# Layer 1 feed-forward of a two-layer diffusion backbone: seven block products for gate and up, down summed in PSUM

## The chip, the core and the metric

The kernel runs on one core of one Trainium2 chip. The time is the device time of an execution in microseconds (us), the median of several runs. The engines are TensorE (PE, matmuls), VectorE (DVE), ScalarE (ACT), GpSimd (POOL) and the DMA queues, here all issued from SyncE (SP). Each engine goes through its own list of instructions in order and waits on semaphores for the others.

## The reference

A network of two layers on 512 latent tokens and 256 context tokens of width 1024, all in float32. Layer 0 mixes tokens by differential attention, layer 1 by grouped-query attention; behind each stands a gated feed-forward of hidden width 2816. Only the latent tokens leave layer 1, so its feed-forward runs on 512 tokens:

```
def swiglu(t, w_gu, w_down):
    gate, up = jnp.split(t @ w_gu, 2, axis=-1)
    return (jax.nn.silu(gate) * up) @ w_down
```

Its input `t` is the RMS-normed and modulated residual stream `x`, and its output is multiplied by a gate vector and added to `x`.

## The kernel before

Every float32 matrix is split into a high part (a cast to the matmul's type) and a low part (source minus high part), and every product is three matmuls, high x high, high x low and low x high. The high parts are cast on ACT, the low parts are subtracted on POOL (weights) or DVE (activations).

`ffn` (L369) serves both layers. The hidden width is cut in 22 chunks of 128 columns, worked in 11 pieces of two. For a chunk, `load` fetches 1 MB of gate and up weights into one of three raw buffers, `stage` splits them (ACT L86, POOL L93), and `gu_mm` sums gate and up over eight blocks of the width for all 512 tokens (L433: 2 x 8 x 3 matmuls of 512 columns; the first two chunks go in halves of 256 columns, since the last token block isn't normed yet when they start). ACT applies silu (L478), DVE multiplies by up (L479), ACT and DVE split the result (L490, L493). `down` then multiplies a piece by its two blocks of w_down (L100 to L102, through `mm3`), for each of four token blocks and two halves of the width, and DVE multiplies each result by the gate vector (L386) and adds it to `x` (L387): 88 such pairs in layer 1. PSUM is three pools of two buffers: S (two banks each), P and T (one bank each).

Ahead of it stands the output projection of the attention (L361, L365 on DVE). After each token block `mk_after` starts the norm (`norm_a`, scaling on L297), and one block later `norm_b` transposes it (L307), modulates it (L322 on DVE, L324 on ACT) and splits it into `h3` (L327, L328). The last block's norm is finished inside `ffn`, by the callback `mid` after the first products of chunk 0. `store` (L1133) writes the output.

The program is written in this order, but a scheduler rearranges it for each engine by its own estimate of times (`schedule_with_timeline_sim=True`, L1180), so the order of rows on an engine is read from the built program, not from the code.

## Time and profile before

| | us |
|---|---|
| median of 3 runs | 1746.75 (1746.62 to 1749.67) |
| span of the profiled execution | 1742.5 |
| median less span | 4.25 |
| TensorE busy | 1657.0 (95%) |
| VectorE, GpSimd, ScalarE busy | 1237.5, 767.6, 673.0 |
| layer 1's feed-forward, first unbroken matmul to end | 1366.6 to 1742.5 |

The page counts the busy time of each engine over the whole span. To judge one stage one goes to views cut to its stretch: windows (busy time in a stretch), groups by line, the timeline of one engine, and the chain of waits, which is followed back from the last instruction. A matmul's own duration in the timeline is longer than its pace, because matmuls overlap; the pace is read from the distance of starts. The clock that TensorE was granted stands as a share of full speed: 1.00 is 2.4 GHz, 0.50 is 1.2 GHz.

### The profile page before, as it was taken

What the parts mean: (1) busy time and instruction counts of PE and PEld (TensorE: products, weight loads), DVE (VectorE), ACT (ScalarE), POOL (GpSimd) and SP (SyncE); (2) the same over time, 40 slices, a digit from 0 to 9 for tenths busy, and PEclk for the clock granted to TensorE, in tenths of its full rate; (3) what the DMA queues carried; (4) which work ended last, traced back from release to release, by engine and by line L of the source; (5) the groups of instructions that cost most, each with busy time, mean ns of one, the idle gap of its engine ahead of it and who ended that gap; (6) DMA issues with size and microseconds to landing.
All of it is one profiled execution on the core that took longest, in us unless ns stands there. A gap on an engine that the chain in (4) does not pass through costs nothing.

```text
span 1742.5 us, 23575 instructions
## 1 busy us (share of the span) xinstructions
PE 1657.0 (95%) x8934; PEld 1403.6 (81%) x8934; DVE 1237.5 (71%) x2016; ACT 673.0 (39%) x1491; POOL 767.6 (44%) x702
## 2 busy tenths in 40 slices
PE   5899999989998999999999999999999999999998
PEld 2789899975778888887777888778897888888887
DVE  4777888877484488878777555798883467677676
ACT  4667767677444121111211022364673522222120
POOL 2687666664645242223232233174435344354340
PEclk8899999999999999999999999999999999999999
DMA  8311111129523133355333221021203133233311
GB/s 303 102 55 38 46 46 58 34 75 336 195 73 121 49 121 111 107 169 169 122 119 99 73 73 40 25 74 48 73 25 120 36 105 103 73 97 99 95 49 49
DMA packets 162435, 165.81 MB, mean 95 GB/s; under 512 B 5097, under 2 KB 120186, under 8 KB 162322
## 3 DMA queue, kind: packets, MB, share of 16 engines
q1 hardware_dynamic: 162322, 164.31, 29.5%
q8 instruction: 70, 1.15, 0.3%
q14 instruction: 43, 0.35, 0.1%
HBM read 159.81 MB, written 4.48 MB: 94 GB/s over the span
## 4 chain that ended last, share of the span: by engine, by line
PE 68%; DVE 18%; ACT 4%; DMA 4%; POOL 3%; issue 2%; SPq 0%; DVEq 0%; ACTq 0%; POOLq 0%
PE psgu L433 24%; PE psgc L433 5%; PE psd L100 5%; PE psd L102 5%; PE psd L101 5%; DVE adacc L225 3%; DMA adaw<-in_ada_w_dram 3%; PE psp L100 2%; PE psp L102 2%; PE psp L101 2%; DVE adacc L223 2%; DVE x L387 2%; DVE xd L386 1%; PE pso L100 1%; PE pso L102 1%
## 5 line engine op out<-in xcount | busy, mean ns | idle before, releaser
L93 POOL TENSOR_TENSOR gul<-gu,guh 128x2048 fp32r<-128x2048 f32 x44 | 211.6, 4809 | 419.6 <-ACT guh L86 419.6
L386 DVE TENSOR_TENSOR xd<-psd,gate 128x512 f32<-128x512 f32 x220 | 151.1, 687 | 202.7 <-PE psd L102 202.5
L387 DVE TENSOR_TENSOR x<-x,xd 128x512 f32<-128x512 f32 x220 | 274.4, 1249 | 5.5
L86 ACT CAST guh<-gu 128x2048 fp32r<-128x2048 f32 x44 | 83.9, 1906 | 403.8 <-PE psgu L433 234.4
L91 POOL TENSOR_TENSOR dl<-wd,dh 128x1024 fp32r<-128x1024 f32 x44 | 120.9, 2768 | 146.1 <-ACT dh L86 146.1
L433 PE MATMUL psgu<-h3latl,guh 128*128 128x512 f32 (+1 forms) x384 | 144.5, 377 | 1.1 <-POOL h3latl L328 1.1
L433 PE MATMUL psgu<-h3lath,gul 128*128 128x512 f32 (+1 forms) x384 | 144.4, 376 | 0.0
L433 PE MATMUL psgu<-h3lath,guh 128*128 128x512 f32 (+1 forms) x384 | 144.3, 377 | 0.0
L433 PE MATMUL psgu<-h2lath,guh 128*128 128x512 f32 (+1 forms) x368 | 142.1, 386 | 0.0
L433 PE MATMUL psgu<-h2lath,gul 128*128 128x512 f32 (+1 forms) x368 | 141.8, 385 | 0.0
L433 PE MATMUL psgu<-h2latl,guh 128*128 128x512 f32 (+1 forms) x368 | 141.8, 385 | 0.0
L100 PE MATMUL psd<-dh,ah 128*128 128x512 f32 x264 | 106.0, 402 | 16.2 <-DVE xd L386 12.1
L102 PE MATMUL psd<-dh,al 128*128 128x512 f32 x264 | 104.8, 397 | 0.0
L101 PE MATMUL psd<-dl,ah 128*128 128x512 f32 x264 | 104.5, 396 | 0.0
L433 PE MATMUL psgc<-h2ctxh,gul 128*128 128x256 f32 x352 | 100.2, 285 | 0.4 <-POOL gul L93 0.4
L433 PE MATMUL psgc<-h2ctxh,guh 128*128 128x256 f32 x352 | 100.1, 284 | 0.0
L433 PE MATMUL psgc<-h2ctxl,guh 128*128 128x256 f32 x352 | 99.6, 283 | 0.0
L225 DVE SCALAR_TENSOR_TENSOR adacc<-adaw,cond,adacc 128x512 f32<-128x512 f32 x112 | 97.5, 896 | 1.3
L100 PE MATMUL psp<-dwh,h0lath 128*128 128x384 f32 x256 | 88.9, 347 | 7.6 <-DVE vl L97 7.6
L101 PE MATMUL psp<-dwl,h0lath 128*128 128x384 f32 x256 | 88.9, 347 | 0.0
L102 PE MATMUL psp<-dwh,h0latl 128*128 128x384 f32 x256 | 88.8, 347 | 0.0
L433 PEld LDWEIGHTS psgu<-h3latl,guh 128*128 128x128 f32 x384 | 72.2, 188 | 15.8 <-POOL h3latl L328 1.3
(389 smaller groups left out, 4669.1 us busy)
## 6 DMA issues: line engine op xcount, KB each, us to landing
adaw<-in_ada_w_dram SPq DMA_DIRECT2D x48, 1024.0 KB
gu<-in_ffn_w_gu_dram SPq DMA_DIRECT2D x88, 512.0 KB
wd<-in_ffn_w_down_dram SPq DMA_DIRECT2D x22, 1024.0 KB
dw<-in_diff_w_in_dram SPq DMA_DIRECT2D x48, 256.0 KB
x<-in_x_dram SPq DMA_DIRECT2D x8, 512.0 KB
wo<-in_diff_w_out_dram SPq DMA_DIRECT2D x4, 1024.0 KB
gw<-in_gqa_w_in_dram SPq DMA_DIRECT2D x4, 1024.0 KB
wo<-in_gqa_w_out_dram SPq DMA_DIRECT2D x4, 1024.0 KB
```

Of the source, the lines that this page charges most:

```text
L86: S.copy(hi, src)
L91: G.tensor_sub(lo[:, ns], src[:, ns], hi[:, ns])
L93: G.tensor_sub(lo[:, :, ns], src[:, :, ns], hi[:, :, ns])
L100: PE.matmul(ps, lhi, rhi, start=start, stop=False)
L101: PE.matmul(ps, lhi, rlo, start=False, stop=False)
L102: PE.matmul(ps, llo, rhi, start=False, stop=stop)
L223: V.tensor_scalar(acc, w[:, k, :], c, None, op0=ALU.mult)
L225: V.scalar_tensor_tensor(acc, w[:, k, :], c, acc, op0=ALU.mult, op1=ALU.add)
L386: V.tensor_mul(tmp, ps, gates[g][:, s, cs])
L387: last_v[0] = V.tensor_add(xt[tb][:, cs], xt[tb][:, cs], tmp)
L433: last[0] = PE.matmul(o, w_[:, k, us], act.t[kind][x_].k(k, sl_), start=(k == 0 and x_ == 0 and w_ is whi), stop=(k == KC - 1 and w_ is wlo))
```

## The change

Only layer 1's feed-forward changes in what it does. Layer 0 and both attentions keep their code, but for the order of two buffers.

`ffn` is replaced by `ffn_up` and `ffn_down`. For gate and up the tokens are cut in two halves of 256 (blocks 0 and 1, blocks 2 and 3), the width in two halves of 512, and the two output halves are gate and up. The 2 x 2 by 2 x 2 block product is made of seven products (Strassen's, in Winograd's form) in place of eight. Weight operands: four blocks as they are and three sums (`prep`, L583 and L584 on POOL, L586 and L588 on DVE). Token operands: b11, b21, b22 as they are and the combinations t1 to t4, which need blocks of both halves (`Forms.done`, L371 to L376, all on DVE). Each operand is split in high and low: for weights L594 on ACT, L595 on DVE (on POOL for product 4); for tokens L351 on ACT, L352 on DVE or POOL. A product is 12 matmuls of 256 columns (L626). The results are put together while they accumulate in PSUM (copies L632, L637, L639 and silu L635, L642 on ACT; L634, L641, L644, L645, L648 on DVE). Products 1 and 2 of chunks 0 to 2 stand ahead of the last norm (`product_order`, `mid` at `None`). The gated activations are written to DRAM (`put`).

`ffn_down` then goes over all 22 chunks twice, once per half of the tokens: it reads the activations back (four chunks at a time), splits them (L669, L670), loads w_down two chunks at a time, splits it (L678 on ACT, L679 on POOL), and sums over all chunks in PSUM, so that the gate multiply and the add to `x` (L702, L703) come once for each block and half of the width.

```diff
+        def done(self, xs, tb, banks=None):
+            ht = norm_mod(xs, norm_t(xs, tb, self.l, 1, banks), tb, self.l, 1)
+            half = 0 if tb in self.halves[0] else 1
+            j = self.halves[half].index(tb)
+            lo, hi = ht[:, 0:4, :], ht[:, 4:8, :]
+            self.ht[half, j] = (lo, hi)
+            if half == 0:
+                self.put("b11", j, lo, V)
+                self.put("b21", j, hi, G)
+            else:
+                b11, b21 = self.ht[0, j]
+                self.put("b22", j, hi, G)
+                V.tensor_sub(b11, lo, b11)
+                self.put("t1", j, b11, V)
+                V.tensor_sub(lo, hi, lo)
+                V.tensor_sub(hi, hi, b11)
+                self.put("t2", j, hi, G)
+                V.tensor_sub(b21, b21, hi)
+                self.put("t3", j, lo, V)
+                self.put("t4", j, b21, G)
...
+    RHS = {1: "b11", 2: "b21", 3: "b22", 4: "t4", 5: "t1", 6: "t2", 7: "t3"}
+    PLEAD = 7
+
+    def product_order():
+        o = [(0, 1), (0, 2), (1, 1), (1, 2), None, (2, 1), (2, 2), (0, 5), (0, 6), (0, 3), (0, 7), (1, 5), (0, 4), (1, 6), (1, 3), (1, 7)]
+        o += [(1, 4), (2, 5), (2, 6), (2, 3), (2, 7)]
+        for h in range(3, NHC):
+            o += [(h, 1), (h - 1, 4), (h, 2), (h, 5), (h, 6), (h, 3), (h, 7)]
+        return o + [(NHC - 1, 4)]
...
+        def prep(hc, n):
+            w = raw[hc]
+            r11, r12, r21, r22 = [w[:, k : k + 4, u : u + P] for u in (0, P) for k in (0, 4)]
+            s1 = st_tile(hc)
+            if n == 5:
+                adds[0].tensor_add(s1, r21, r22)
+                adds[1].tensor_sub(r21, r11, r21)
+            elif n == 6:
+                adds[2].tensor_sub(r11, s1, r11)
+            elif n == 3:
+                adds[3].tensor_sub(r12, r12, r11)
+            src = {1: r11, 2: r12, 5: s1, 6: r11, 3: r12, 7: r21, 4: r22}[n]
+            if not wq:
+                t = slab("w", F32R, f"wf{l}_{hc}_{n}", 2).rearrange("p a (x k n) -> p a x k n", x=2, k=4)
+                wq.extend([t[:, 0], t[:, 1]])
+            t = wform[hc, n] = wq.pop(0)
+            S.copy(t[:, 0], src)
+            (G if n == 4 else V).tensor_sub(t[:, 1], src, t[:, 0])
+            if n == 4:
+                load(hc + 3)
...
+            w, x = wform.pop((hc, n)), F.tiles[RHS[n]]
+            for k in range(4):
+                for a_, b_ in ((0, 0), (0, 1), (1, 0)):
+                    last_m[0] = PE.matmul(
+                        ps, w[:, a_, k, :], x[:, b_, k, :],
+                        start=(n in (1, 2, 5) and k == 0 and a_ + b_ == 0),
+                        stop=(k == 3 and a_ == 1), skip_group_check=n in (3, 4, 6, 7))
+            c1, c2, c5, g1, g2, u2 = [ev[hc][:, e * th : e * th + th] for e in range(6)]
+            if n == 1:
+                S.copy(c1, ps)
+            elif n == 2:
+                V.tensor_add(g1, ps, c1)
+                S.activation(g1, g1, AF.Silu)
+            elif n == 5:
+                S.copy(c5, ps)
+            elif n == 6:
+                S.copy(c2, ps)
+            elif n == 3:
+                V.tensor_add(g2, ps, c2)
+                S.activation(g2, g2, AF.Silu)
+            elif n == 7:
+                V.tensor_add(u2, ps, c5)
+                last_v[0] = V.tensor_mul(g2, g2, u2)
+                puts.append((i, hc, 1, g2))
+            else:
+                last_v[0] = V.tensor_mul(g1, g1, ps)
+                puts.append((i, hc, 0, g1))
...
+                if k % 4 == 0:
+                    n = min(4, NHC - k)
+                    r = raw_tile(f"ar{l}_{half}_{k}", 4, th)[:, :n]
+                    dma(r, a_dram[k : k + n, :, half, :].rearrange("k p n -> p k n"))
+                    t = a_tile(half, k).rearrange("p (x k n) -> p x k n", x=2, k=4)
+                    S.copy(t[:, 0, :n], r)
+                    V.tensor_sub(t[:, 1, :n], r, t[:, 0, :n])
+                    for e in range(n):
+                        aw[k + e] = (t[:, 0, e], t[:, 1, e])
+                if k % 2 == 0:
+                    r = raw_tile(f"wd{l}_{half}_{k}", 2, D)
+                    dma(r, w_down[l, k * P : (k + 2) * P, :].rearrange("(k p) n -> p k n", p=P))
+                    ww["raw"] = r
+                t = slab("w", F32R, f"wd{l}_{half}_{k}x", 2)
+                S.copy(t[:, 0], ww["raw"][:, k % 2])
+                lo_eng.tensor_sub(t[:, 1], ww["raw"][:, k % 2], t[:, 0])
+                ww[k] = (t[:, 0], t[:, 1])
...
+            def out(tb, ch):
+                s = 0 if tb < NLAT else 1
+                cs = slice(ch * 512, ch * 512 + 512)
+                tmp = xtp.tile([P, 512], F32, tag="xtmp", name=f"xd{l}_{tb}_{ch}")
+                V.tensor_mul(tmp, ps[tb][ch], gates[g][:, s, cs])
+                last_v[0] = V.tensor_add(xt[tb][:, cs], xt[tb][:, cs], tmp)
+                after(tb, ch)
...
-    h3 = Act("h3", ("dd", "ee"))
-    after = mk_after(1, 1, h3, 1, ("f", "xc"), NLAT - 1)
+    HALVES1 = ([0, 1], [2, 3])
+    TH1 = 2 * P
+    form1 = lambda n, t: slab(t, F32R, f"hf1{n}", 2).rearrange("p x (k n) -> p x k n", k=4)
+    F1 = Forms(1, HALVES1, {n: form1(n, t) for n, t in (("b11", "e"), ("b21", "e"), ("b22", "g"), ("t1", "g"), ("t2", "d"), ("t3", "d"), ("t4", "k"))})
+    after = mk_after(
+        1, 1, slots(["xc", "f"], "11"), lambda xs, tb: F1.done(xs, tb), 1, NLAT - 1)
     out_proj(wto, wtags, xt, oT1, lat, gw_out[0], gates[1, 0], "1", after, {})
-    tags1 = dict(gu="gk", a=None, al="l", sil="l")
+    st1 = slab("k", F32, "st1").rearrange("p (s k n) -> p s k n", s=4, k=4)
+    a1 = dram.tile([NHC, P, 2, TH1], F32, name="a1")
+    ffn_up(
+        1, F1, lambda hc: slab("l", F32, f"ev1_{hc}"), lambda hc: st1[:, hc % 4], a1, (G, G, V, V),
+        lambda: after(None, True))
...
-    ffn(1, xt, h3, lat, (1, 1), tags1, lambda: after(None, True), None, [], store)
+    ffn_down(
+        1, xt, HALVES1, (1, 1), a1, lambda half, k: slab("l", F32R, f"a21_{half}_{k}"),
+        (("S", "S"), ("P", "T")), G, lambda half, k: None, store)
```

The order of the rows. The names: `wf_h_n` is the split weight operand of chunk h (a tile holds two operands), `gu_h` its raw weights, `st` the tile of sums, `psu` and `psc` PSUM, `ev` the evacuated results, `hf1b` and `hf1t` the split token operands.

First DVE at the start of the feed-forward. Before, from the last add of the projection to the last block's low halves:

```order
L365 TENSOR_TENSOR x_6176<-x_6176,xo_13492 128x512
L322 TENSOR_SCALAR xs11xc<-pt_13543,modA,mod_128 128x128 x4
L328 TENSOR_TENSOR h3latl_13151<-xs11f,h3lath_13149 128x4x128
L112 TENSOR_SCALAR m_n_13497<-ss_13495 128x1
L328 TENSOR_TENSOR h3latl_13151<-xs11xc,h3lath_13149 128x4x128
L105 TENSOR_TENSOR m_n_13497<-m_n_13497,r_n_13498 128x1
L106 SCALAR_TENSOR_TENSOR m_n_13497<-m_n_13497,r_n_13498 128x1
L107 SCALAR_TENSOR_TENSOR r_n_13498<-m_n_13497,r_n_13498 128x1
L297 TENSOR_SCALAR xs11xc<-x_6176,r_n_13498 128x1024
L322 TENSOR_SCALAR xs11xc<-pt_13565,modA,mod_128 128x128 x4
L328 TENSOR_TENSOR h3latl_13151<-xs11xc,h3lath_13149 128x4x128
L479 TENSOR_TENSOR sil_13717<-sil_13717,psgu_0_13518 128x512
```

After, in the middle of the same stretch, with the last block's modulation (L325) and the rows up to t1's last low half (the last row; `hf1t_13151` is t1):

```order
L325 TENSOR_SCALAR xs_0_13436<-pt_13644,modA,mod_128 128x128 x3
L595 TENSOR_TENSOR wf_0_3_13559<-gu_0_13511,wf_0_3_13559 128x512
L325 TENSOR_SCALAR xs_0_13436<-pt_13644,modA,mod_128 128x128
L595 TENSOR_TENSOR wf_1_5_13595<-st_13509,wf_1_5_13595 128x512
L376 TENSOR_TENSOR xs_1_13335<-xs_1_13335,xs_0_13436 128x512
L371 TENSOR_TENSOR xs_1_13335<-xs_0_13436,xs_1_13335 128x512
L595 TENSOR_TENSOR wf_1_6_13682<-gu_1_13514,wf_1_6_13682 128x512
L634 TENSOR_TENSOR ev_2_13687<-psu_2b,ev_2_13687 128x256
L595 TENSOR_TENSOR wf_1_6_13682<-gu_1_13514,wf_1_6_13682 128x512
L373 TENSOR_TENSOR xs_0_13436<-xs_0_13436 128x512
L352 TENSOR_TENSOR hf1t_13153<-xs_0_13436,hf1t_13153 128x4x128
L352 TENSOR_TENSOR hf1t_13151<-xs_1_13335,hf1t_13151 128x4x128
```

Weight operands, evacuations and combinations of tokens now stand in one row with the last norm.

Next PE at the start. Before, around the transposes of the last block:

```order
L433 MATMUL psgu_1_13620<-h3latl_13151,guh_1_13616 128x256
L433 MATMUL psgu_1_13620<-h3lath_13149,gul_1_13617 128x256
L307 MATMUL pt_13565<-ident,xs11xc 128x128 x4
L307 MATMUL pt_13570<-ident,xs11xc 128x128 x4
L433 MATMUL psgu_1_13620<-h3lath_13149,guh_1_13616 128x256
```

After, the same place (`pt_13644` and `pt_13649` are the last block's transposes):

```order
L626 MATMUL psu_0_13543<-hf1b_13149,wf_0_1_13520 128x256 x12
L626 MATMUL psu_1_13578<-hf1b_13149,wf_1_1_13525 128x256 x12
L310 MATMUL pt_13644<-ident,xs_0_13436 128x128 x4
L626 MATMUL psu_2a<-hf1b_13148,wf_2_1_13530 128x256
L310 MATMUL pt_13649<-ident,xs_0_13436 128x128 x4
L626 MATMUL psu_2a<-hf1b_13148,wf_2_1_13530 128x256 x5
L626 MATMUL psc_0_13721<-hf1t_13151,wf_0_5_13537 128x256
L626 MATMUL psc_1_13793<-hf1t_13151,wf_1_5_13595 128x256
L626 MATMUL psc_0_13721<-hf1t_13151,wf_0_5_13537 128x256 x11
```

Behind the last product of chunk 2 that needs the first half of the tokens, the next row already needs t1 (`hf1t_13151`).

Last DVE in the middle of the loop. Before, beside chunks 16 and 17:

```order
L479 TENSOR_TENSOR sil_13717<-sil_13717,psgu_16_15251 128x512
L386 TENSOR_TENSOR xd_7_0_1_15326<-psd_7_0_1_15319,gate_12144 128x512
L387 TENSOR_TENSOR x_6173<-x_6173,xd_7_0_1_15326 128x512
L493 TENSOR_TENSOR a_8_15302<-sil_13717,a_8_15302 128x512
L386 TENSOR_TENSOR xd_7_1_0_15336<-psd_7_1_0_15329,gate_12144 128x512
L387 TENSOR_TENSOR x_6173<-x_6173,xd_7_1_0_15336 128x512
L386 TENSOR_TENSOR xd_7_1_1_15346<-psd_7_1_1_15339,gate_12144 128x512
L387 TENSOR_TENSOR x_6173<-x_6173,xd_7_1_1_15346 128x512
L386 TENSOR_TENSOR xd_7_2_0_15356<-psd_7_2_0_15349,gate_12144 128x512
L387 TENSOR_TENSOR x_6176<-x_6176,xd_7_2_0_15356 128x512
```

After, beside chunks 11 to 13:

```order
L648 TENSOR_TENSOR ev_11_14957<-ev_11_14957,psu_11_14956 128x256
L595 TENSOR_TENSOR wf_13_2_15094<-gu_13_14829,wf_13_2_15094 128x512
L595 TENSOR_TENSOR wf_13_2_15094<-st_13509,wf_13_2_15094 128x512
L588 TENSOR_TENSOR gu_13_14829<-gu_13_14829 128x4x128
L595 TENSOR_TENSOR wf_13_6_15130<-gu_13_14829,wf_13_6_15130 128x512
L641 TENSOR_TENSOR ev_12_15080<-psc_12_15134,ev_12_15080 128x256
L595 TENSOR_TENSOR wf_13_6_15130<-gu_13_14829,wf_13_6_15130 128x512
L644 TENSOR_TENSOR ev_12_15080<-psu_12_15079,ev_12_15080 128x256
L645 TENSOR_TENSOR ev_12_15080<-ev_12_15080 128x256
L595 TENSOR_TENSOR wf_13_7_15164<-gu_13_14829,wf_13_7_15164 128x512
L595 TENSOR_TENSOR wf_13_7_15164<-gu_14_14953,wf_13_7_15164 128x512
L634 TENSOR_TENSOR ev_13_15204<-psu_13_15203,ev_13_15204 128x256
```

The residual's multiplies and adds are gone from the loop; low halves of weights (L595) stand in their place, and between them rows that wait for a product in PSUM.

## Rows read from the trace of the kernel before

**Rows 1.** The page: busy us, share of the span and instructions of each engine.
```profile
PE 1657.0 (95%) x8934; PEld 1403.6 (81%) x8934; DVE 1237.5 (71%) x2016; ACT 673.0 (39%) x1491; POOL 767.6 (44%) x702
```

**Rows 2.** Timeline of PE, start of layer 1's feed-forward: start, us, then line and operation.
```profile
1366.62 0.39 PE L433 MATMUL psgu<-h3latl,guh 128*128 128x256 f32 x1 [1.11 <-POOL h3latl L328]
1366.84 0.28 PE L433 MATMUL psgu<-h3lath,gul 128*128 128x256 f32 x1
...
1372.53 0.28 PE L433 MATMUL psgu<-h3lath,gul 128*128 128x256 f32 x1
```

**Rows 3.** Timeline of PE, its last matmul.
```profile
1737.67 0.40 PE L102 MATMUL psd<-dh,a 128*128 128x512 f32 x1
```

**Rows 4.** Windows, layer 1's feed-forward: us, busy by engine (instructions), PEclk, DMA share, GB/s.
```profile
1430.00:1700.00 270.00, 270.00 (x1159) 217.31 (x1158) 192.28 (x162) 63.75 (x64) 120.34 (x34) 1.00 0.30 89
```

**Rows 5.** Chain of waits in 1560 to 1600: shares by line, then start, us, what.
```profile
by line: PE psgu L433 71.8%; PE psd L102 9.9%; PE psd L101 9.3%; PE psd L100 9.3%
...
1560.14 9.80 PE psgu L433 x42
```

**Rows 6.** Tile h3latl, one operation on two engines: min/median/max ns, first and last start.
```profile
L328 POOL TENSOR_TENSOR h3latl<-xs11f,h3lath x2: 1290/1504/1717, 1357.7 to 1364.8; 128x512 fp32r<-128x512 f32 x2
L328 DVE TENSOR_TENSOR h3latl<-xs11f,h3lath x2: 680/680/680, 1359.4 to 1366.6; 128x512 fp32r<-128x512 f32 x2
...
L328 DVE TENSOR_TENSOR h3latl<-xs11xc,h3lath x2: 1360/1366/1371, 1368.9 to 1377.6; 128x512 fp32r<-128x512 f32 x2
```

**Rows 7.** Timelines of DVE and of POOL around 1560 to 1579.
```profile
1562.36 5.70 POOL L91 TENSOR_TENSOR dl<-wd,dh 128x1024 fp32r<-128x1024 f32 x2
1571.77 4.62 POOL L93 TENSOR_TENSOR gul<-gu,guh 128x2048 fp32r<-128x2048 f32 x1 [3.72 <-ACT guh L86]
...
1562.90 0.68 DVE L386 TENSOR_TENSOR xd<-psd,gate 128x512 f32<-128x512 f32 x1
1572.10 4.84 DVE L387 TENSOR_TENSOR x<-x,xd 128x512 f32<-128x512 f32 x1
1578.17 0.69 DVE L387 TENSOR_TENSOR x<-x,xd 128x512 f32<-128x512 f32 x1
1578.78 0.69 DVE L493 TENSOR_TENSOR a<-sil,a 128x512 fp32r<-128x512 f32 x1
```

**Rows 8.** Groups by line in 1430 to 1700: count, busy us, mean ns, idle before.
```profile
L387 DVE TENSOR_TENSOR x<-x,xd 128x512 f32<-128x512 f32 x64 | 118.3, 1848 | 1.7
```

**Rows 9.** Line L97, a DVE subtraction that reads PSUM, 128x256.
```profile
L97 DVE TENSOR_TENSOR oT1latl<-pgo,oT1lath x16: 411/425/427, 1233.8 to 1324.1; 128x256 fp32r<-128x256 f32 x16
```

**Rows 10.** Timeline of DVE between the last projection and the last block's modulation.
```profile
1364.03 0.68 DVE L361 TENSOR_TENSOR xo<-pso,gate 128x512 f32<-128x512 f32 x1
1370.76 0.75 DVE L297 TENSOR_SCALAR xs11xc<-x,r_n 128x1024 f32<-128x1024 f32 x1
1374.60 1.37 DVE L322 TENSOR_SCALAR xs11xc<-pt,modA,mod 128x128 f32<-128x128 f32 x4 [3.08 <-PE pt L307]
```

**Rows 11.** PE's idle at 528.8 (timeline) and the granted clock behind it (windows).
```profile
533.67 0.69 PE L307 MATMUL pt<-ident,xs01f 128*128 128x128 f32 x2 [4.87 <-DVE m_n L112]
539.00:540.00 1.00, 1.00 (x7) 1.00 (x7) 1.00 (x3) 1.00 (x4) 0.04 (x1) 0.50 0.00 0
541.00:542.00 1.00, 1.00 (x11) 1.00 (x10) 0.50 (x1) 1.00 (x2) 0.97 (x1) 1.00 0.00 0
800.00:810.00 10.00, 7.31 (x38) 5.92 (x37) 5.44 (x5) 2.77 (x3) 4.56 (x1) 1.00 0.60 214
```

**Rows 12.** A load of 1 MB and its cast, two splits (timelines), a crowded stretch (windows).
```profile
624.40 0.99 SPq L55 DMA_DIRECT2D gu<-in_ffn_w_gu_dram  x2
630.12 1.91 ACT L86 CAST guh<-gu 128x2048 fp32r<-128x2048 f32 x1 [9.47 <-DMA gu<-in_ffn_w_gu_dram]
1318.83 4.77 POOL L91 TENSOR_TENSOR dl<-wd,dh 128x1024 fp32r<-128x1024 f32 x2 [5.90 <-ACT dh L86]
400.00:410.00 10.00, 10.00 (x74) 6.04 (x76) 7.85 (x20) 7.30 (x20) 9.41 (x19) 1.00 1.03 370
```

More of the change, by code (lines that the diff above doesn't have):

```diff
@@ L298, in norm_a, with norm_t @@
         return xs
-    def norm_t(xs, tb, l, which):
+    def norm_t(xs, tb, l, which, banks=None):
         pts = []
@@ L303, in norm_t @@
             nm = f"pt{l}{which}{tb}{q}"
-            pt = psb(nm, "T") if q or l + which == 2 else ps2(nm)[:, 0, :]
+            if banks:
+                pt = psb(nm, banks)
+            else:
+                pt = psb(nm, "T") if q or l + which == 2 else ps2(nm)[:, 0, :]
             pts.append(pt.rearrange("p (k n) -> p k n", n=P))
@@ L308, in norm_t, with norm_mod @@
         return pts
-    last_v, last_s = [None], [None]
-    def norm_m(xs, src, tb, l, which, hi, lo, nv=4):
+    last_v, last_s, last_m = [None], [None], [None]
+    def norm_mod(xs, src, tb, l, which, nv=4):
         s = 0 if tb < NLAT else 1
@@ L324, in norm_m @@
                         S.activation(ht[:, k, :], x_, AF.Identity, bias=b, scale=a)
+        return ht
+    def norm_m(xs, src, tb, l, which, hi, lo, nv=4):
+        ht = norm_mod(xs, src, tb, l, which, nv)
         for q in range(2):
@@ L328, in norm_m, with norm_b, __init__, put @@
             last_v[0] = (V if q else G).tensor_sub(lo.q(q), ht[:, qs, :], hi.q(q))
-    def norm_b(xs, tb, l, which, hi, lo):
-        norm_m(xs, norm_t(xs, tb, l, which), tb, l, which, hi, lo)
+    def norm_b(xs, tb, l, which, hi, lo, banks=None):
+        norm_m(xs, norm_t(xs, tb, l, which, banks), tb, l, which, hi, lo)
+    class Forms:
+        def __init__(self, l, halves, tiles):
+            self.l, self.halves, self.tiles, self.ht, self.late = l, halves, tiles, {}, []
+        def put(self, name, j, src, eng):
+            if name not in self.tiles:
+                self.late.append((name, j, src, eng))
+                return
+            t, cs = self.tiles[name], slice(j * P, j * P + P)
+            S.copy(t[:, 0, :, cs], src)
+            last_v[0] = eng.tensor_sub(t[:, 1, :, cs], src, t[:, 0, :, cs])
+        def rest(self, tiles):
+            self.tiles.update(tiles)
+            for a in sorted(self.late, key=lambda a: a[0]):
+                self.put(*a)
+        def done(self, xs, tb, banks=None):
[18 more added lines that the diff above has]
+                self.put("t4", j, b21, G)
     def o_weights(wt, tags, w_dram, nm, ch):
@@ new lines, in ffn_down, with prep, mms @@
+    def ffn_down(l, xt, halves, g, a_dram, a_tile, banks, lo_eng, step, after):
+        th = len(halves[0]) * P
+        for half, tbs in enumerate(halves):
+            items, aw, ww = [], {}, {}
+            def prep(k):
+                if k >= NHC:
+                    return
+                if k % 4 == 0:
[15 more added lines that the diff above has]
+                ww[k] = (t[:, 0], t[:, 1])
+            for k in range(3):
+                prep(k)
+            ps = {}
+            for j, tb in enumerate(tbs):
+                b = banks[half][j]
+                if b == "S":
+                    t = ps2(f"psd{l}_{tb}")
+                    ps[tb] = [t[:, 0, :], t[:, 1, :]]
+                else:
+                    ps[tb] = [psb(f"psd{l}_{tb}_{ch}", b) for ch in range(2)]
+            def mms(k, tb, ch):
+                j = tbs.index(tb)
+                ts_, cs = slice(j * P, j * P + P), slice(ch * 512, ch * 512 + 512)
+                mm3(ps[tb][ch], aw[k][0][:, ts_], aw[k][1][:, ts_], ww[k][0][:, cs], ww[k][1][:, cs], k == 0, k == NHC - 1)
+            def out(tb, ch):
[5 more added lines that the diff above has]
+                after(tb, ch)
+            TAIL = 2
+            for k in range(NHC - TAIL):
+                prep(k + 3)
+                for tb in tbs:
+                    for ch in range(2):
+                        mms(k, tb, ch)
+                step(half, k)
+            for tb in tbs:
+                for ch in range(2):
+                    for k in range(NHC - TAIL, NHC):
+                        mms(k, tb, ch)
+                    out(tb, ch)
```

68 lines of the change are left out of this document (55 added, 13 removed).

## The prediction

> **What bounds the kernel now.** I read the page first: TensorE (PE) is busy 95% of the span and VectorE (DVE) 71% [rows 1]. Those shares are averages over stages, so I went to the stage that is changed, the feed-forward of layer 1. Its unbroken run begins at 1366.62 us, with an L433 matmul behind a wait of 1.1 us [rows 2], and its last matmul starts at 1737.67 [rows 3]. In 1430 to 1700 the windows view has PE busy 270.00 of 270 us, DVE 192.28, ACT 63.75, POOL 120.34, DMA at 89 GB/s [rows 4], and the chain of waits there consists of matmuls only [rows 5]. So PE sets the time of this stage, 371.5 us (1366.62 to about 1738.1), and every other engine has slack, DVE 78 us in 270.
>
> The engines beside PE matter all the same, because the change hands them work. Here the reader should look at pairs of rows. A subtraction of 128x512 with both inputs in SBUF takes 0.68 us on DVE and 1.29 on POOL when alone; begun during the other's, DVE's takes 1.36 and POOL's 1.72 [rows 6]. The residual add `x<-x,xd` (two SBUF inputs) takes 0.69 us in the quiet and 4.84 beside a POOL operation of 4.62, but `xd<-psd,gate`, whose first input is PSUM, takes 0.68 us at 1562.90, in the middle of POOL's 1562.36 to 1568.06 [rows 7]. I read this as: a DVE operation on two SBUF inputs and a POOL operation exclude each other, and a DVE operation that reads PSUM is free. That is how L387 comes to a mean of 1848 ns here [rows 8].
>
> **What the change takes from PE.** Before, a chunk of the hidden width costs 2x8x3 = 48 matmuls of 512 columns at 0.2333 us (42 in 9.80 us [rows 5]): 11.2 us. After, seven products of 4x3 = 12 matmuls of 256 columns, 84 in all. Their pace, each with new weights, stands in the startup of before: 48 steps from 1366.84 to 1372.53 [rows 2], 0.1186 us, so 9.96 a chunk. The first two chunks of before run at 256 columns already (96 x 0.1186 = 11.4 each). Over 22 chunks 246.8 becomes 219.1. Down is 528 matmuls of 512 columns in both kernels, 123.2 us. PE's bare sum, with 0.9 us of transposes: 343.2 us against 371.5, less 28.
>
> **What it adds in the up loop: forms and evacuations.** By the order of rows two chunks cost DVE 26 operations: 16 of 128x512 on two SBUF inputs (12 low halves L595, the additions L586 and L588), 2 of 128x256 in SBUF (L645) and 8 of 128x256 from PSUM (L634, L641, L644, L648). Back to back the first kind paces 0.61 us (1578.17 to 1578.78 [rows 7]): 9.8; the PSUM kind lasts 0.425 [rows 9]: 3.4; the L645 have no row, I take them at 0.4, between half of 0.69 and a PSUM one: 0.8. POOL gets six of 128x512 (L583, L584, one L595 a chunk): 6 x 1.29 = 7.7. If nothing coincides that is 21.7 us; if all eight PSUM reads lie beside POOL, 18.3; PE needs 19.92. So DVE and POOL together, with much of their time free before, become as long as PE. Neither bound is reached, since the engines wait for each other at short distance: L648 waits for a chunk's last product and frees the bank that PE wants one product (1.42 us) later, L644 and L634 two products, and each stands in DVE's row among forms. I take 20.65, a little above the middle of 18.3 and 21.7: 0.7 more than PE, over the 10.6 pairs left after the first six products 7.5 us of PE idle (bounds 0 and 18.9). ACT isn't in question: 7 casts a chunk, each a quarter of the tile that takes 1.91 [rows 12], three copies and two activations.
>
> **What it adds at the start: a hole.** Six products (chunks 0 to 2, operands b11 and b21) need token blocks 0 and 1 only; all others need t1 to t4 or b22, which exist only once block 3 is normed, transposed, modulated and combined. Before, the last `xo` multiply starts at 1364.03, block 3 is scaled by 1371.51, and PE has other work until it is ready [rows 2, 10]. After, DVE does four more SBUF operations in between (L586, L588, two L595), behind weight casts of ACT that need the projection's slots: some 2 us, so block 3 is scaled near 1373.6. The low half of b11's second block, which gates the first full product, falls near 1371. The six products (72 x 0.1186 = 8.5 us, and transposes) end near 1380.7. From the scaling to t1's last low half DVE has 22 rows: 14 SBUF operations of 512 (0.64 on average, with the dependent ones), two sets of modulation at 1.37 [rows 10], three evacuations: 13.0 us if it never waits, thus 1386.6. POOL has six operations there (7.7 us) that exclude the 14; some fall into DVE's own waits. So t1 is whole between 1386.6 and 1394.3; I take 1392, towards the late end, since two of the evacuations wait for the second products of chunks 0 and 1. Without a hole PE would be at that point at 1366.62 + 9.5 = 1376.1: 15.9 us lost (bounds 10.5 and 18.2), some 11 of them one idle stretch.
>
> **Clock.** PE's idle of 4.87 us before 533.67 is followed by a granted clock of 0.50, which is 1.2 GHz, still in 539 to 540 with PE at work, and by 1.00 from 541 [rows 11]. A hole of 11 us will do the same: about 3 us of work at half pace, 1.5 lost, of which I take half as hidden, for DVE and POOL are behind at that point: 0.8.
>
> **Down.** Sums stay in PSUM over all chunks, so 88 pairs of L386 and L387 become 8 (L702, L703), and DVE matters no more. In exchange w_down is loaded, cast and split once for each half of the tokens. Per four chunks PE needs 11.2 us and POOL 4 x 2.39 = 9.5 (two in 4.77 [rows 12]); the DMAs move 2.5 MB, 230 GB/s against 370 in a crowded stretch [rows 12]. A raw slot is held for a load (5.7 us, 624.40 to 630.12 [rows 12]), the first half's cast (half of 1.91 [rows 12]) and the splits (4.8): 11.5 us against 11.2, 0.3 x 11 = 3.3, less 2.6 of prefetch under the last products: 0.7 (0 to 11, the upper end with splits at 2.85, two in 5.70 [rows 7]). The activations' trip through DRAM (44 writes, 12 reads) lies beside PE; at the turn from up to down the first chunks were written long before. The tail from 1737.67 on is the same.
>
> **Sum.** 343.2 + 15.9 + 0.8 + 7.5 + 0.7 = 368.1 against 371.5: 3.4 us less on a span of 1742.5. The median, 1746.75, lies 4.25 us above that span, which I carry over: 1743.4, say 1743.5. The gain of 28 us goes to the hole and the up loop nearly whole.
>
> **Rivals.**
> B, DVE keeps up. PSUM reads coincide with POOL, a pair costs PE's own 19.92, and t1 comes near 1388: 7.5 + 4 less, 1732. For it: alternation wastes little, two splits of 4.77 alone take 5.70 around DVE's work [rows 7, 12]. Against it: both engines keep to their rows, and DVE isn't ahead after the hole.
> C, DVE and POOL one after the other, slower. Nothing coincides: 21.7 a pair, 18.9 us of idle, and t1 at 1394: 11.4 + 2 more than forecast, 1757. From 21.3 a pair on it is slower than before by more than 0.2%. For it: L387's mean shows how often the two collide already [rows 8].
> D, the weight slots set the pace of down, slower: splits at 2.85 make a slot 12.4 us, 1.2 x 11 less 2.6, 10.6, so 10 more, 1753.5. Against it: DVE is nearly idle there, so POOL runs alone.
> E, PE's short waits halve its clock within the up loop. In this trace 2.7 us of idle in 800 to 810 left it at 1.00 [rows 11], so I give it little: 3 us at 1.2 GHz a pair would cost 1.5 x 10.6 = 16, 1759.5. The Trainium skill ("TensorE: Matmul & The Clock Gate", section "A second HAM failure mode: psum-queue depth-cycling") speaks for this rival: it tells of a kernel whose PE idled briefly between groups of matmuls as PSUM banks were cycled, so that the clock went back and forth between its levels. By that rule the time would be E's; the row of 800 to 810 speaks against it here.
> F, the change doesn't do what it says, as when the weight reads for the first chunks come late: the hole grows as the loop shrinks, 1746.
>
> **How the numbers follow.** A, the forecast (1743.5, own range 1737 to 1751), 0.50: of it faster 0.23, same 0.17, slower 0.10. B 0.22, faster. C 0.15, D 0.06, E 0.04, slower. F 0.03, same. A difference of 0.2%, 3.5 us, is about what a measurement of this kernel can tell from no change. Faster 0.45, same 0.20, slower 0.35. Below 1727 (B with a hole some 5 us shorter still) lie about 0.08, above 1762 (C with the ring's cost, E) about 0.1: that is the range.
>
> **What would show it.** Right: PE idle 9 to 13 us in one piece after six products, near 1381 to 1392, with a granted clock of 0.5 behind it; then L626 waiting for L595, L634, L644 or L648, some 0.7 us a pair; DVE near full in the up loop; PE busy all through down. Wrong: a hole under 5 us, or no waits in the up loop (B); DVE's and POOL's busy times that add up to the loop's length (C); PE waiting for POOL's splits L679 (D); a granted clock under 1 in the up loop (E). The forecast fails most easily by the length of a pair: 0.33 us of it is the whole gain.

## The result, and the profile after

The changed kernel takes 1768.36 us (median of 4 runs, 1763.68 to 1770.05) beside 1747.47 of before (4 runs): the ratio is 1.0108, 95% interval 1.009 to 1.0126. It is slower by 21 us (1.1%), where 1743.5 was forecast. PE's work did shrink, and its busy share of the span fell from 95% [rows 1] to 93%. From the page:

```profile
PE 1647.9 (93%) x9630; PEld 1432.1 (81%) x9630; DVE 1236.3 (70%) x2120; ACT 768.7 (43%) x1729; POOL 820.6 (46%) x772
```

The profiled span is 1768.3 us against 1742.5. I read it from the front. The last matmul of layer 1's output projection starts at 1363.0 before and at 1372.72 now, so 9.7 us are lost ahead of everything that the prediction costed. PE's timeline behind it (start, length, line, operation, in brackets the idle time before and what ended it):

```profile
1372.72 0.39 PE L102 MATMUL pso<-woh,oT1latl 128*128 128x512 f32 x1
...
1377.91 0.79 PE L626 MATMUL psu<-hf1b,wf 128*128 128x256 f32 x2 [3.93 <-ACT hf1b L351]
...
1389.08 0.84 PE L626 MATMUL psu_2a<-hf1b,wf 128*128 128x256 f32 x5
1397.00 0.80 PE L626 MATMUL psc<-hf1t,wf 128*128 128x256 f32 x2 [7.08 <-ACT hf1t L351]
1402.36 5.06 PE L626 MATMUL psc<-hf1t,wf 128*128 128x256 f32 x22 [4.56 <-DVE hf1t L352]
```

This is the forecast hole: PE is through its six products by 1390, waits 7.08 and 4.56 us, and then runs 22 matmuls in 4.85 us (the next row starts at 1407.21) where the full pace, 0.1186 each, would take 2.61. The windows agree (us, busy by engine with instructions, granted clock, DMA share, GB/s):

```profile
1390.00:1400.00 10.00, 0.80 (x2) 0.50 (x2) 10.00 (x14) 7.88 (x18) 6.86 (x4) 0.73 0.38 105
1400.00:1410.00 10.00, 7.64 (x42) 7.65 (x43) 4.11 (x5) 2.46 (x5) 5.83 (x5) 0.58 0.00 0
1430.00:1600.00 170.00, 161.13 (x1315) 158.69 (x1314) 138.61 (x205) 89.87 (x189) 70.87 (x47) 0.99 0.43 122
```

The last row is the up loop: PE is no longer full there, as it was in [rows 4]. Its waits, once a pair of chunks:

```profile
1477.46 1.69 PE L626 MATMUL psu<-hf1b,wf 128*128 128x256 f32 x12 [0.95 <-DVE ev L648]
1499.82 1.70 PE L626 MATMUL psu<-hf1b,wf 128*128 128x256 f32 x12 [1.70 <-DVE ev L648]
1522.19 1.70 PE L626 MATMUL psu<-hf1b,wf 128*128 128x256 f32 x12 [1.70 <-DVE ev L648]
1544.25 2.43 PE L626 MATMUL psu<-hf1b,wf 128*128 128x256 f32 x12 [1.75 <-DVE ev L648]
```

The starts lie 22.36, 22.37 and 22.06 us apart; PE's own work is 19.92. What DVE and POOL do just ahead of the second of these waits:

```profile
1494.60 1.45 DVE L586 TENSOR_TENSOR gu<-st,gu 128x512 f32<-128x512 f32 x1
1495.98 1.78 DVE L595 TENSOR_TENSOR wf<-gu,wf 128x512 fp32r<-128x512 f32 x1
1497.79 1.64 DVE L588 TENSOR_TENSOR gu<-gu 128x512 f32<-128x512 f32 x1
1499.36 0.41 DVE L648 TENSOR_TENSOR ev<-ev,psu 128x256 f32<-128x256 f32 x1
...
1493.88 1.62 POOL L583 TENSOR_TENSOR st<-gu 128x512 f32<-128x512 f32 x1 [5.82 <-DMA gu<-in_ffn_w_gu_dram]
1495.58 1.63 POOL L584 TENSOR_TENSOR gu<-gu 128x512 f32<-128x512 f32 x1
1497.16 1.72 POOL L595 TENSOR_TENSOR wf<-gu,wf 128x512 fp32r<-128x512 f32 x1
```

As soon as a chunk's weights land, POOL has three operations in a row. Three of DVE's with both inputs in SBUF, 0.68 us when alone, take 1.45, 1.78 and 1.64, and each ends 0.55 us behind the end of one of POOL's (1495.50, 1497.21, 1498.88). L648 stands behind them, and PE waits for L648. The Trainium skill ("SBUF — State Buffer", section "SBUF: two separate sides") states this as an exclusive lock: whichever of a two-SBUF-input DVE instruction and a GpSimd instruction starts first holds the shared ports for its whole length. These rows agree.

### The profile page after: what moved, and what is told of

Same layout as the page of the kernel before. It is cut to its first block, busy times and chain, and to the rows that moved or that the text cites. A ratio compares the mean times of both kernels' runs of the same rounds, so it can differ in the third digit from the quotient of the medians.

```text
span 1768.3 us, 25718 instructions
## 1 busy us (share of the span) xinstructions
PE 1647.9 (93%) x9630; PEld 1432.1 (81%) x9630; DVE 1236.3 (70%) x2120; ACT 768.7 (43%) x1729; POOL 820.6 (46%) x772
## 4 chain that ended last, share of the span: by engine, by line
PE 57%; DVE 23%; DMA 7%; ACT 5%; POOL 4%; issue 4%; SPq 1%; DVEq 0%; ACTq 0%; POOLq 0%
PE psgu L480 11%; PE psu L626 5%; PE psgc L480 5%; PE psd L100 3%; PE psd L101 3%; PE psd L102 3%; DMA adaw<-in_ada_w_dram 3%; DVE adacc L225 3%; PE psc L626 3%; PE psp L100 2%; PE psp L102 2%; PE psp L101 2%; DVE wf L595 2%; DVE adacc L223 2%; DMA wd<-in_ffn_w_down_dram 1%
## 5 line engine op out<-in xcount | busy, mean ns | idle before, releaser
L93 POOL TENSOR_TENSOR gul<-gu,guh 128x2048 fp32r<-128x2048 f32 x22 | 109.3, 4968 | 235.9 <-ACT guh L86 228.1
L433 DVE TENSOR_TENSOR xd<-psd,gate 128x512 f32<-128x512 f32 x132 | 90.7, 688 | 112.5 <-PE psd L102 112.5
L86 ACT CAST guh<-gu 128x2048 fp32r<-128x2048 f32 x22 | 41.9, 1906 | 213.4 <-PE psgu L480 125.1
L434 DVE TENSOR_TENSOR x<-x,xd 128x512 f32<-128x512 f32 x132 | 130.6, 991 | 3.2
L91 POOL TENSOR_TENSOR dl<-wd,dh 128x1024 fp32r<-128x1024 f32 x22 | 60.0, 2744 | 140.1 <-ACT dh L86 140.1
L595 DVE TENSOR_TENSOR wf<-gu,wf 128x512 fp32r<-128x512 f32 x110 | 95.5, 884 | 12.5 <-ACT wf L594 12.4
L594 ACT CAST wf<-gu 128x512 fp32r<-128x512 f32 x132 | 78.3, 619 | 57.5 <-PE psu L626 32.4
L626 PE MATMUL psu<-hf1t,wf 128*128 128x256 f32 x756 | 98.5, 283 | 2.4 <-DVE ev L644 1.6
L626 PEld LDWEIGHTS psu<-hf1t,wf 128*128 128x128 f32 x756 | 93.9, 190 | 3.5 <-DVE ev L644 2.0
L583 POOL TENSOR_TENSOR st<-gu 128x512 f32<-128x512 f32 x22 | 32.3, 1472 | 120.7 <-DMA gu<-in_ffn_w_gu_dram 97.2
```

Of the source, the lines that this page charges most:

```text
L91: G.tensor_sub(lo[:, ns], src[:, ns], hi[:, ns])
L93: G.tensor_sub(lo[:, :, ns], src[:, :, ns], hi[:, :, ns])
L433: V.tensor_mul(tmp, ps, gates[g][:, s, cs])
L434: last_v[0] = V.tensor_add(xt[tb][:, cs], xt[tb][:, cs], tmp)
L594: S.copy(t[:, 0], src)
L595: (G if n == 4 else V).tensor_sub(t[:, 1], src, t[:, 0])
```

## The experiments

Times are medians, ratios go against runs of the kernel before on the same chip. "The stage" below is from the start of the projection's last matmul to the span's end: 379.5 us in the profile of before, 395.6 after.

**Both kernels again.** Edit: none.

> The kernel before, unchanged, for a second trace of it on the chip that the next runs use. Expected: the marks of the trace ahead of layer 1's feed-forward (last matmul of layer 0's projections psp 374.1 us, first output projection of layer 0 468.1, last matmul of layer 1's output projection 1363.0) within 1.5 us of the first trace. If these marks move by 5 us or more from execution to execution, part of the 9.7 us by which the changed kernel is late there is chance.

> The changed kernel, unchanged, for a second trace. Theory one (the rows ahead of the feed-forward really became slower, by the order that the scheduler gives them): last output projection of layer 1 again near 1372.7 us, 9 to 10 us later than in the kernel before. Theory two (chance): near 1364 to 1368, and the total near 1762 to 1766. In both, the hole of 12 us after the six products and a pair of chunks near 21.8 us in the up loop should be seen again.

One execution each: 1745.1 and 1772.68. The holes repeat to 0.01 us (7.09 and 4.57), the stage takes 378.1 and 396.0, and the projection's last matmul starts at 1365.2 and 1374.9, again 9.7 apart (in before it is 2.2 later than in the first trace, where 1.5 was expected at most). So the losses in the stage belong to the program, not to one execution.

**A fourth raw buffer** (raw4x). Theory R: the loads, not DVE, set the pace.

```diff
-                w = raw[hc] = raw_tile(f"gu{l}_{hc}", KC, 256)
+                w = raw[hc] = slab("xc", F32, f"gux{l}_{hc}", KC) if hc > 3 and hc % 4 == 3 else raw_tile(f"gu{l}_{hc}", KC, 256)
...
+                load(hc + 4)
```

> Gate and up weights get a fourth raw buffer (every fourth chunk from chunk 7 on is loaded into a tile that is free by then) and loads are begun one chunk earlier; the work of DVE, POOL and ACT is the same. Theory R (the ring of raw buffers): in the trace of the changed kernel a load is issued only when POOL has done product 4's low half, which stands behind the two sums of the chunk that has just arrived, so that one load, two sums and a low half follow each other: 5.9 + 1.45 + 1.62 + 1.72 = 10.7 us a chunk, 21.4 a pair, against 19.9 of PE. With the fourth buffer the pair falls to 20.0 to 20.6 and the kernel gains 10 to 17 us against the changed one. Theory X (DVE and POOL exclude each other, the working of the forecast): the pair stays at 21.5 to 22 and the time within 3 us of the changed kernel.

1768.45 us, ratio 1.0098 (1.0074 to 1.0121). The loop's last `psu` matmul starts at 1635.9 against 1636.4, with the same waits for L634 and L648. Theory R falls.

**No POOL in the up loop** (n4addv). Weight sums and product 4's low halves go to DVE.

```diff
-            (G if n == 4 else V).tensor_sub(t[:, 1], src, t[:, 0])
+            V.tensor_sub(t[:, 1], src, t[:, 0])
...
-(G, G, V, V),
+(V, V, V, V),
```

> All weight sums and all low halves of weights on DVE, none on POOL, raw buffers as in the changed kernel. Theory X: DVE's own work in a pair is 22 x 0.61 + 0.8 + 3.4 = 17.6 us, nothing excludes it, so the pair falls to PE's 19.9 to 20.3 and the kernel gains 14 to 18 us. Theory R: the loop becomes a load of 5.9 and three DVE operations of 0.6 with waits in DVE's row between them, 8 to 10 us a chunk: a gain too, 10 to 18 us; with raw4x the two theories are told apart. If the pair grows beyond 21.8, DVE's row is the bound and both are wrong.

1760.95 us, ratio 1.0056 (1.0037 to 1.0076); the stage takes 384.9, 10.7 less. PE's waits in the loop sum to 4.1 us, against 11.2. The windows view, 1430 to 1600, of this kernel beside the row of after above:

```profile
1430.00:1600.00 170.00, 166.09 (x1364) 163.46 (x1363) 138.35 (x262) 91.17 (x194) 0.00 (x0) 1.00 0.44 125
```

DVE does 262 instructions in 138.35 us busy where it did 205 in 138.61 while POOL worked 70.87 us. POOL's 47 operations cost DVE as much, in time shut out, as doing them itself.

The gain over the changed kernel is 7.4 us, half of the 14 to 18 expected. One pair takes 20.14 (1510.38 to 1530.52), but earlier ones still wait, up to 1.52 us. And since DVE is equally busy in both kernels, PE doesn't wait for the amount of DVE's work but for where it lies. The edit also gives DVE another order of rows (most waits are now for L634); how much of the gain is the exclusion and how much the order wasn't tested apart.

**Low halves of w_down on DVE** (lov). Theory D: POOL's splits hold down back.

```diff
-        (("S", "S"), ("P", "T")), G, lambda half, k: None, store)
+        (("S", "S"), ("P", "T")), V, lambda half, k: None, store)
```

> The low halves of w_down on DVE instead of POOL in the second pass, all else as in the changed kernel. Theory D (POOL's splits and the raw slots hold PE up in down): PE's idle time there falls from 5.5 us to under 2, and the kernel gains 3 to 5 us. If the loads alone hold it up, the idle time stays at 4 to 6 us.

1760.81 us, ratio 1.0071 (1.005 to 1.0092), 7.6 less than the changed kernel, where 3 to 5 were expected; the stage takes 388.7, 6.9 less. In after the weight loads of down wait (total, times, longest us):

```profile
PEld psd L101 <- POOL wd_8x L679: 1.7, 1, 1.7
PEld psd L101 <- POOL wd_12x L679: 1.2, 1, 1.2
PEld psd L100 <- ACT wd_8x L678: 1.2, 1, 1.2
```

and 110 us of it show PE short of full:

```profile
1642.00:1752.00 110.00, 106.57 (x454) 84.38 (x453) 29.49 (x18) 45.48 (x46) 96.74 (x38) 1.00 0.62 223
```

With DVE splitting, those waits are gone:

```profile
1643.00:1753.00 110.00, 110.00 (x475) 89.19 (x474) 62.63 (x58) 48.46 (x49) 0.00 (x0) 1.00 0.63 224
```

The tail shrinks too, which wasn't expected. In after the four last results stand in PSUM together, and DVE's eight operations run behind each other from 1760.08 on:

```profile
1760.08 1.29 DVE L702 TENSOR_TENSOR xd<-psd,gate 128x512 f32<-128x512 f32 x2 [12.11 <-PE psd L102]
1761.29 1.28 DVE L703 TENSOR_TENSOR x<-x,xd 128x512 f32<-128x512 f32 x2
1762.48 1.28 DVE L702 TENSOR_TENSOR xd<-psd,gate 128x512 f32<-128x512 f32 x2
1763.68 1.29 DVE L703 TENSOR_TENSOR x<-x,xd 128x512 f32<-128x512 f32 x2
```

From the last matmul's start to the span's end are 7.3 us (1761.03 to 1768.3). Without POOL the scheduler sets the last matmuls so that the results end one after the other, and it is 5.6 (1757.54 to 1763.1).

**The old order of slots** (slotsold). Theory S: the exchanged order of two pairs of norm buffers changes what the scheduler does ahead of the stage.

```diff
-slots(["g", "f"], "01", True)
+slots(["f", "g"], "01", True)
...
-slots(["w", "f"], "10", True)
+slots(["f", "w"], "10", True)
```

> The changed kernel with only the order of the two slots of the scaled rows as in the kernel before, in layer 0's second norm and layer 1's first (f before g, f before w). With it the rows of PE, DVE and ACT up to layer 1's output projection stand as before; the feed-forward is the changed one. Theory S (the slot order moved rows of layer 1's projection and attention): the last matmul of layer 1's output projection comes back from 1373 to 1364 to 1369 us and the kernel gains 4 to 9 us against the changed one (1768). Theory P (the 9.5 us come from DVE operations shut out by POOL at places that the row order doesn't decide): it stays at 1371 to 1375, gain under 2 us.

1762.49 us, ratio 1.0079 (1.0057 to 1.01). The projection's last matmul starts at 1365.8, 7 us earlier (2.0 of them are there already at the end of layer 0's input projections), and the stage is 2.9 shorter (392.7). Theory S's mark and its gain are both met.

**The new order in the kernel before** (beforeslots), the same exchange alone.

```diff
-    after = mk_after(0, 1, h2, 1, "fg", NLAT - 1)
+    after = mk_after(0, 1, h2, 1, "gf", NLAT - 1)
...
-            h1.append(mk_after(1, 0, h1[0], 1, "fw"))
+            h1.append(mk_after(1, 0, h1[0], 1, "wf"))
```

> The kernel before with nothing changed but the order in which two norms take their pairs of buffers (g ahead of f behind layer 0's attention, w ahead of f behind layer 0's feed-forward), the order that the changed kernel has. Theory S (that order alone makes the scheduler arrange layer 0's end and layer 1's attention worse, and costs the 5 to 7 us ahead of the feed-forward that the old order took off the changed kernel): last matmul of layer 1's output projection 5 to 7 us later than 1363.0 to 1365.2, median 1751.5 to 1754 beside some 1747 of before. Rival: the old order helped the changed kernel only through what the scheduler did with the new feed-forward's forms behind it; then before doesn't move by more than 2 us.

1752.73 us (8 runs) against 1748.24, ratio 1.0024 (1.0014 to 1.0035). The projection's last matmul starts at 1369.0, 3.8 to 6.0 later than in the two profiles of before; but 3.2 of that are there already at the end of layer 0's input projections, far ahead of the exchange. A cleaner measure is layer 1's attention, from the last matmul of layer 0's feed-forward to the last of the projection: 239.9 us, against 235.2 and 236.7 in before. So the order costs by itself some 4 us, and theory S holds at the lower end of what it expected. Windows over 1190 to 1250 show where: the first row is before, the second before with the new order, the third after, the fourth after with the old order.

```profile
1190.00:1250.00 60.00, 57.11 (x328) 48.77 (x327) 52.23 (x137) 32.50 (x75) 26.21 (x39) 1.00 0.15 53
```
```profile
1190.00:1250.00 60.00, 54.30 (x289) 45.80 (x288) 49.16 (x123) 28.33 (x65) 24.75 (x37) 0.94 0.13 36
```
```profile
1190.00:1250.00 60.00, 54.30 (x276) 45.38 (x275) 50.12 (x131) 25.84 (x59) 23.87 (x36) 0.94 0.12 36
```
```profile
1190.00:1250.00 60.00, 57.09 (x326) 48.52 (x325) 51.50 (x137) 32.52 (x76) 25.26 (x38) 1.00 0.16 53
```

Either kernel loses 2.8 us of PE there with the new order, and its clock dips.

**A shorter lead of weight operands at the start** (lead3).

```diff
-            while nprep <= min(i + PLEAD, len(preps) - 1):
+            while nprep <= min(i + (3 if i < 8 else PLEAD), len(preps) - 1):
```

> Weight operands are prepared three products ahead in place of seven until product 5 of chunk 0; nothing else. Theory H (the hole behind the six products is DVE's row of forms, in which five low halves of weights stand ahead of t1): t1 is whole 3 to 4 us earlier, and the hole (12.5 us of idle in two pieces) falls to 8 to 10; since DVE has to do those rows later, in a loop without slack, the kernel gains only 0 to 3 us. If the hole stays at 12 us or more, transposes and modulation set it, and not the weights.

1768.98 us, ratio 1.0111 (1.0091 to 1.0131), hole 7.09 and 4.64: nothing. The scheduler put the same weight rows ahead of t1 all the same, so this did not test what it was meant to.

**The four edits together** (comb2): no POOL in the loop, low halves of w_down on DVE, old slots, shorter lead.

> Together: slots as in slotsold, no POOL in the up loop (as n4addv), w_down's low halves on DVE (as lov), three products of lead at the start (as lead3). Sum of the single expectations: 4 to 9 + 7.4 (measured for n4addv) + 3 to 5 + 3 to 4, since DVE has slack now: 17 to 25 us less than the changed kernel, 1743 to 1751, that is from the time of the kernel before (1747 to 1749) to 6 us under it. If exclusion by POOL was what spent the gain, the waits of PE for L634, L644 and L648 nearly vanish (under 4 us in all).

1750.14 us (12 runs), ratio 1.0007 (0.9996 to 1.0018), level with before, within the 17 to 25 us expected under the changed kernel. The stage takes 380.6, 15 less than after; the single gains in it add up to 20.5, so they overlap.

**t1 first** (comb3). To that kernel one thing is added: weights' low halves that stood ahead of t1's last one on DVE are ordered behind it.

```diff
+            if name == "t1":
+                self.t1 = last_v[0]
...
-            V.tensor_sub(t[:, 1], src, t[:, 0])
+            with tc.issue_after(F.t1.ins) if 7 <= nprep <= 14 else nullcontext():
+                V.tensor_sub(t[:, 1], src, t[:, 0])
```

> This is comb2 (weight sums and product 4's low half on DVE, low halves of w_down on DVE, the old order of slots, PLEAD 3) with one thing more: the low halves of the weight operands that stand ahead of t1's last low half on DVE (wf_0_3, wf_1_5, wf_1_6) are put behind it. Theory H (the hole behind the six products is DVE's work up to t1, and the weights' rows in it are part of that): five rows of 0.65 to 1.5 us go behind, t1 is whole 3 to 4 us earlier, the hole of 7.1 + 3.8 us in comb2 shrinks to 7 to 9 us in all, and the median falls from comb2's 1750.1 to 1745.5 to 1747.5, level with before or just under it. Rival: t1 is set by the chain of the last norm (transposes, modulation, PE's second products), DVE's weight rows fill its waits only; then the hole stays at 10.5 to 11.5 and the median at 1749 to 1751.5. A second rival: t1 comes earlier but wf_1_5 and wf_1_6 come too late for products 5 and 6, so that the wait moves behind t1: hole 7 to 9 us, new waits of 2 to 4 us at L626 on wf, same median.

1744.01 us (7 runs), ratio 0.9971 (0.9958 to 0.9984): 0.3% under before, little but clear of noise. PE's timeline at the hole, first of the four edits, then with t1 first:

```profile
1392.31 0.80 PE L626 MATMUL psc<-hf1t,wf 128*128 128x256 f32 x2 [7.08 <-ACT hf1t L351]
1396.89 5.00 PE L626 MATMUL psc<-hf1t,wf 128*128 128x256 f32 x22 [3.79 <-DVE hf1t L352]
```
```profile
1391.20 3.84 PE L629 MATMUL psc<-hf1t,wf 128*128 128x256 f32 x14 [7.08 <-ACT hf1t L351]
1395.61 2.50 PE L629 MATMUL psc<-hf1t,wf 128*128 128x256 f32 x10 [0.56 <-DVE wf L598]
```

The second wait, which was DVE's weight rows, is gone but for 0.56; the first, 7.08, was left as it is, so there theory H fails. Its rival, that the last norm's chain sets this wait, is not shown either: ACT's and PE's rows stand in that chain too, as the section on the prediction tells, and no run moved them. The rest of the gain is in the loop, where PE's windows row now reads:

```profile
1430.00:1600.00 170.00, 169.22 (x1402) 167.73 (x1402) 141.24 (x268) 95.68 (x200) 0.00 (x0) 1.00 0.45 130
```

Why the loop's last short waits went with the reordering wasn't tested apart.

**Token low halves on DVE too** (comb4).

```diff
-                self.put("b21", j, hi, G)
+                self.put("b21", j, hi, V)
```

and so for b22, t2 and t4.

> This is comb3 with the token operands' low halves b21, b22, t2, t4 (L352) on DVE in place of POOL, so that POOL has nothing to do around the hole. Theory X (a DVE operation on two SBUF inputs and a POOL operation shut each other out) taken strictly: moving a row from POOL to DVE then costs nothing, since either way DVE stands for it, and saves POOL's slower pace (1.29 us against 0.65): the stretch to t1 gets up to 2 to 4 us shorter than in comb3, median 1743 to 1746. Rival: POOL's rows mostly lay in DVE's waits for transposes and PSUM, so that DVE now has up to 8 rows of 0.65 more in the stretch, of which some 4 stand ahead of t1: hole 2 to 3 us longer than comb3's, median 1747 to 1750.

1744.8 us (11 runs), ratio 0.9975 (0.9966 to 0.9984), hole 7.07 and 0.86: the same as without it. Neither the gain nor the loss that was expected came: here too a POOL operation and its move to DVE are worth the same.

## Why the prediction was wrong, point by point

The predicted span, 1739.1, missed 1768.3 by 29.2 us: 9.7 ahead of the stage, 19.5 in it. By the medians the miss is 24.9: the profiled span of before lies 4.25 us under its median and that of after only 0.1, so some 4 us of the 29.2 come from the pair of executions.

**Ahead of the stage: a step that failed by omission.** The part ahead was taken as unchanged without a word: the sum began at 1366.62. The exchanged order of two pairs of buffers, seen in the diff, moved rows there. Layer 1's attention, from the last matmul of layer 0's feed-forward to the last of the projection, takes 235.2 to 237.1 us in all six profiles with the old order and 239.9 to 240.6 in all seven with the new one. Between before and after that is 5.1 of the 9.7. Another 1.0 lies ahead of it, behind layer 0's input projections. The other 3.6 lie up to the end of those, where the order of rows on DVE, ACT and POOL is the same in all kernels: that part ends at 374.1 in both profiles of before, at 377.8 and 379.0 in those of after, and over all profiles anywhere from 374.1 to 380.0. Some 2.6 of the 3.6 go with the DVE row of the last section. Whether this is scatter between executions or belongs to the program stays open.

**PE's bare work: right.** 343.2 us was forecast; a product's 12 matmuls start 1.43 us apart in the loop against 1.42, 1.0 us over the loop. 27 us were saved.

**The hole: right in its end, in part by luck.** PE gets going again at 1402.36, 9.7 less is 1392.7; 1392 was forecast for t1. But the forecast counted DVE's and POOL's rows alone. The second wait was DVE's, as the reordered kernel shows; the first ends with a cast on ACT. Behind the last block's scaling (L297) PE goes on with other rows for 6 us before it transposes the block, and ACT has a table load, silu and weight casts in its row ahead of its half of the modulation (L327):

```profile
1381.48 0.76 DVE L297 TENSOR_SCALAR xs<-x,r_n 128x1024 f32<-128x1024 f32 x1
...
1388.16 0.60 PE L310 MATMUL pt<-ident,xs 128*128 128x128 f32 x4
...
1388.61 1.28 ACT L635 ACT_TABLE_LOAD   x1
1391.58 1.48 ACT L327 ACTIVATE xs<-pt,mod,modA 128x128 f32<-128x128 f32 x4
```

What an earlier transpose or a freer ACT would give wasn't tested.

**The clock behind it: 0.8 forecast, 2.2 measured** for the 22 matmuls at half clock alone (4.85 less 2.61); the 13 behind them, at half clock until 1408.3, lose another 0.5 (2.07 us in place of 1.54), which the loop's sum below contains. The half that I took as hidden wasn't: PE has no wait in these rows.

**The up loop: the term that decided, 7.5 forecast, 18.5 measured.** From 1407.21 to 1636.51 are 229.3 us; 146 products at 12 x 0.1186 make 207.8, and 13 matmuls of down that stand in between 3.0. Of the 18.5 that are left, 11.2 are the idle time of eleven waits and some 2 are half clock. The pair was put at 20.65: DVE's own 14.0 and POOL's 7.7, less 1.05 for PSUM reads of DVE beside POOL. From 1477.46 to 1608.89 six pairs take 131.4, 21.9 each, near rival C's 21.7, taken with 0.15. But the six pairs' windows row doesn't show C's mechanism, two engines that fill the pair one after the other:

```profile
1477.46:1608.89 131.43, 124.36 (x1008) 122.33 (x1009) 105.61 (x157) 69.06 (x145) 53.38 (x37) 0.99 0.44 125
```

DVE is busy 17.6 us a pair, 3.6 more than its own work, and idle 4.3, so it is not near full, which the prediction gave as a sign of being right. The overlap was about right: 6.6 of POOL's 53.4 us lie beside PSUM reads, 1.1 a pair. So C's number came out, but not from C's mechanism. The step that failed is the balance itself: it charged DVE 6.65 for POOL's work, which cost it 3.6, and put DVE's own waits, 4.3, at nothing. By busy time alone DVE, with 17.6 against PE's 19.92, wouldn't hold PE up. What does is where the time falls: POOL's work comes in one burst per chunk, when the load lands, and L648, for which PE waits, stands behind the DVE rows that the burst stretches. The prediction named L648's place, but took such waits as a reason for the middle of the bounds and not as a loss.

**Down: 0.7 forecast, 4.6 measured** (1636.51 to 1761.26 less 515 x 0.2333): the mechanism of rival D at half its size. Most splits last 2.4 us, but about one in four, where DVE splits the activations (L670), takes 2.8 to 3.4, so that "DVE is nearly idle there" was true only on the mean. One such pair, POOL and DVE:

```profile
1736.33 3.41 POOL L679 TENSOR_TENSOR wd_14x<-wd,wd_14x 128x1024 fp32r<-128x1024 f32 x1
...
1735.61 1.86 DVE L670 TENSOR_TENSOR a<-ar,a 128x1024 fp32r<-128x1024 f32 x1 [10.51 <-ACT a L669]
```

**The tail: "the same" was wrong by 2.4.** Last matmul's end to the span's end takes 4.6 before, 7.0 after: summing all chunks in PSUM moves the last four results together to the end.

In sum 0.4 (hole: 0.6 later, two matmuls done in it) + 1.4 (clock) + 11.0 (loop) + 3.9 (down) + 2.4 (tail) = 19.1 of the 19.5; the 1.0 of pace lies within the loop's 11.0. Of the 0.4 left, 0.2 are the last matmul's end in before, which the prediction took from the row (1738.1) and I here from the pace (1737.9). Rival B fell, and F too: the seven products do what they say. Of rival E there is one case in the loop's middle: behind the wait of 1.75 us 12 matmuls take 2.43 us in place of 1.70, and the clock over 10 us is 0.83. After the waits of 0.95 and 1.70, a pair or more earlier, the rows run at full pace. In the second execution of the same kernel, with waits of the same size, the clock stays at 1.00 over the loop. First after, then its second execution:

```profile
1540.00:1550.00 10.00, 8.25 (x56) 8.04 (x56) 6.90 (x9) 3.62 (x8) 4.35 (x3) 0.83 0.42 119
```
```profile
1410.00:1640.00 230.00, 218.75 (x1778) 214.09 (x1777) 181.36 (x266) 121.86 (x249) 92.44 (x62) 1.00 0.44 129
```

So the Trainium skill ("TensorE: Matmul & The Clock Gate", section "A second HAM failure mode: psum-queue depth-cycling"), which tells of a clock that goes back and forth behind such short idles, is borne out only now and then: of six profiles with POOL in the loop three show one such fall each, behind waits of 1.75 to 1.84 us, of four without POOL none.

The range's upper end, 1762, was too low since the loop, down and the slots were late together, each priced as if alone.

## What to carry to other kernels

When DVE and POOL both work on SBUF operands, price POOL's operations as if DVE did them (here 3.6 us a pair for six of them), and don't stop at the sum of busy times: look which operand that the bottleneck waits for stands behind POOL's burst. If DVE alone fits under PE, try it without POOL. When work is moved onto an engine that prepares a late operand, order the late operand first. A change that touches allocation order can move rows far from its own stage: compare the order of rows ahead of it, and price what differs.
